# Splits of block sums one product sooner, seven-product pairs from pair 5 on, activation sums spread over pairs 2 to 4

## Chip, cores and metric

The kernel runs on one core of one Trainium2 chip. The metric is the device time of one execution in microseconds (us), as the median of several runs; lower is better.

## What is computed

A trunk of two layers on 512 tokens of width 1024. Each layer is a mixer sub-layer (four token mixers, gates, an output projection) followed by a gated feed-forward network. Only the second part is touched here:

```python
hf = rms_norm(x, norm_ffn_pre[l])
u = causal_depthwise_conv(hf @ ffn_w_up[l], ffn_conv_w[l], ffn_conv_b[l])   # width 3
gate, val = jnp.split(u, 2, axis=-1)
f = (jax.nn.gelu(gate, approximate=True) * val) @ ffn_w_down[l]
x = x + rms_norm(f, norm_ffn_post[l])
```

`ffn_w_up` is 1024 x 5632: 22 blocks of 128 gate columns and 22 of value columns.

## The kernel before

Every matrix product is made of three matmuls in a reduced float format: weight and activation are each split into a high and a low part (`whi`/`wlo`, `hT_hi`/`hT_lo`), and high x high, high x low and low x high are added up in PSUM. Splitting a weight tile of 128 x 1024 takes two instructions: a copy on ScalarE (ACT) that rounds to the high part, and a subtraction on VectorE (DVE) that leaves the low part. SyncE (SP) loads weights in the order of their use into three buffers `raw`; the split parts go to four buffers each.

The gate-and-value projection of a layer goes by **pairs**: pair i is gate block i and value block i. Pairs 0 and 1 come from `head`. A **whole pair** is two chains of 24 matmuls of 512 columns (tile `ps`). The pairs of the set `SEVEN` use a scheme of block sums instead, which needs seven products of quarter size where eight would be made (`seven`, L1401): each `product` is 12 matmuls of 256 columns into one of the banks `sa`, `sb`, `se`. It needs

- sums of the weights, made on GpSimd (POOL) in `w_seven` (four instructions per pair, L193 to L196) and then split by `halves` (L179 on ACT, L180 on DVE);
- sums of the activation, made once per layer by `forms`, for either half h of the contraction: `ta`, `tb`, `tc`, `td` on DVE (L1360), `te` on POOL (L1371 to L1373), and their splits `t1h`/`t1l` to `t4h`/`t4l` (L324 on ACT, L325 on DVE);
- copies of intermediate sums from a bank to SBUF on ACT (`ca` L1409 and L1416, `cb` L1422), since the next product adds on top of them in the same bank, and three additions on DVE (L1413, L1427, L1432).

Of a seven-product pair five products run in a row; the last two (`four`, `three`) are put off and run between the first products of the next pair (`more`). After each pair `ffn_pair` does the width-3 convolution: two ACT instructions (L1319), four DVE instructions (L1323), a GELU on ACT (L1327) and a product on DVE (L1331). From pair 4 on, each whole pair also splits some finished activations for the next stage (`split_act`, tiles `fh`, `fl`).

In this stage TensorE, ACT and DVE run in the order in which the program writes them, and POOL and SP in theirs; an instruction that waits holds up all behind it on its engine. `w_ahead(n)` writes the splits of the next n weights at that point. The instructions of `forms` are not written at once but queued in `bg`; `pump`, which is called after each product, writes some of them as long as DVE is reckoned to be less than a slack (0.9) behind TensorE. Before the first seven-product pair whatever is left in `bg` is written in one go:

```python
                if i in SEVEN:
                    while bg:
                        bg.popleft()()
                    seven(i)
                    continue
```

Of the kernel before, what the change touches and what calls it, by code (L numbers as in the profile page):

```python
# [21 lines left out]
NP_ = DFF // 128  # L22
# [58 lines left out]
T_G = 4.2  # L81
T_M = 5.7

SEVEN = {i for i in range(4, NP_ - 1) if i % 3}

H_2 = 1.0
H_T = 3.0
# [21 lines left out]
def build(tc, x, wts, prm, gains, cst, out, order=None):  # L109
# [4 lines left out]
    V, A, G, T, SP = nc.vector, nc.scalar, nc.gpsimd, nc.tensor, nc.sync  # L114
    with ExitStack() as ctx:
# [10 lines left out]
        def nm(s):  # L126
            uid[0] += 1
            return f"{s}{uid[0]}"

        def slot(w=512, dt=F32, name="g"):  # L130
            return pg.tile([128, w], dt, tag="g", bufs=NG, name=nm(name))
# [7 lines left out]
        def f(t):  # L139
            return t.bitcast(F32)  # L140
# [64 lines left out]
        def w_split(q, roomy=False):  # L205

            if recording:
                return
            while pos["spl"] <= min(q, len(order) - 1):
                i = pos["spl"]  # L210
                w_dma()
                w = unit_width(order[i][1])
                if order[i][1][0] == "fs":
                    w_seven(i)
                    pos["spl"] += 1
                    w_dma()
                    continue
                r = raw.pop(i)
                if roomy:
                    hs, ls = [], []  # L220
                    for c in range(0, w, 512):
                        n = min(512, w - c)
                        hi, lo = slot(dt=F32R, name="bh"), slot(dt=F32R, name="bl")
                        src = r[c // 512] if isinstance(r, list) else r[:, c:c + n]
                        A.activation(hi[:, :n], src, AF.Copy)
                        V.tensor_tensor(lo[:, :n], src, f(hi[:, :n]), op=ALU.subtract)
                        hs.append(hi)
                        ls.append(lo)
                    parts[i] = (hs, ls)
                else:  # L230
                    hi = pw.tile([128, WMAX], F32R, tag="whi", bufs=NSPL, name=nm("whi"))
                    lo = pw.tile([128, WMAX], F32R, tag="wlo", bufs=NSPL, name=nm("wlo"))
                    for c, s in ((0, r[0]), (512, r[1])) if isinstance(r, list) else ((0, r[:, :w]),):
                        n = 512 if isinstance(r, list) else w
                        A.activation(hi[:, c:c + n], s, AF.Copy)  # L235
                        V.tensor_tensor(lo[:, c:c + n], s, f(hi[:, c:c + n]), op=ALU.subtract)  # L236
                    parts[i] = (hi, lo)
                pos["spl"] += 1
                w_dma()

        def w_ahead(n=NSPL - 1):
            w_split(pos["use"] - 1 + n)

        def w_get(l, key):
            if recording:
                order.append((l, key))
                return nc, nc
            assert order[pos["use"]] == (l, key), (order[pos["use"]], key)
            w_split(pos["use"])
            p = parts.pop(pos["use"])  # L250
            pos["use"] += 1
            return p
# [7 lines left out]
        bg = deque()  # L260

        clk = {"pe": 0.0, "dve": 0.0, "slack": SLACK}
# [4 lines left out]
        def dve(us):  # L267
            clk["dve"] = max(clk["dve"], clk["pe"]) + us
# [50 lines left out]
        def hilo(src, scale=1.0, name="hl"):  # L319
            dve(0.62)  # L320
            hi = slot(dt=F32R, name=name + "h")
            lo = slot(dt=F32R, name=name + "l")
            if scale == 1.0:
                A.activation(hi, src, AF.Copy)  # L324
                V.tensor_tensor(lo, src, f(hi), op=ALU.subtract)  # L325
            else:
                A.activation(hi, src, AF.Copy, scale=scale)
                V.scalar_tensor_tensor(lo, src, scale, f(hi), op0=ALU.mult, op1=ALU.subtract)
            return hi, lo
# [269 lines left out]
        for l in range(L):  # L599
# [58 lines left out]
            for kv, b in enumerate((kcb, vcb)):  # L658
                for g in range(2):
                    t = slot(name="F")  # L660
# [674 lines left out]

            hb = head(l, [("fu", 0), ("fu", NP_), ("fu", 1), ("fu", NP_ + 1)], hooks)
            ffn_order.enter_context(tc.manual_schedule(engines={E_T, E_A, E_V}))
            clk["dve"] = clk["pe"]
            ffn_pair(0, hb[0:2])
            ffn_pair(1, hb[2:4])  # L1340
            hb = None
# [3 lines left out]
            def v2(t):  # L1345
                return t.rearrange("p (k t) -> p k t", k=2)
# [3 lines left out]
            def forms(h):  # L1350
                def block(t, k, q):
                    return f(t[:, k * 4 + h * 2:k * 4 + h * 2 + 2, q * 256:q * 256 + 256])
                hi, lo = (lambda k, q: block(hT_hi, k, q)), (lambda k, q: block(hT_lo, k, q))
                a, b, c, d, e, g = (slot(name="t" + n) for n in "abcdef")
                sub, add = ALU.subtract, ALU.add

                def op(o, x, y, how):
                    def go():
                        dve(0.62)
                        V.tensor_tensor(o, x, y, op=how)  # L1360
                    bg.append(go)
                op(v2(a), hi(0, 1), hi(0, 0), sub)
                op(v2(b), lo(0, 1), lo(0, 0), sub)
                op(a, a, b, add)
                op(v2(c), hi(1, 1), v2(a), sub)
                op(v2(c), v2(c), lo(1, 1), add)
                bg.append(lambda: form["d1"].append(hilo(a, name="t1")))
                op(v2(d), hi(1, 0), v2(c), sub)
                op(v2(d), v2(d), lo(1, 0), add)
                bg.append(lambda: form["d2"].append(hilo(c, name="t2")))  # L1370
                G.tensor_tensor(v2(e), hi(1, 1), hi(0, 1), op=sub)  # L1371
                G.tensor_tensor(v2(g), lo(1, 1), lo(0, 1), op=sub)
                G.tensor_tensor(e, e, g, op=add)  # L1373
                bg.append(lambda: form["d4"].append(hilo(d, name="t4")))
                bg.append(lambda: form["d3"].append(hilo(e, name="t3")))

# [6 lines left out]
            def product(b, w, c, n, first):  # L1383

                o = b[:, 0:256]
                kw = {} if first else {"skip_group_check": True}
                for kt in range(4):
                    hi, lo = side(n, kt)
                    k = c + kt * 128
                    mm(o, wc(w[0], k), hi, first and kt == 0, False, **kw)  # L1390
                    mm(o, wc(w[0], k), lo, False, False, **kw)
                    mm(o, wc(w[1], k), hi, False, kt == 3, **kw)
                pump(1.42)
# [3 lines left out]
            def more():  # L1397
                if rest:
                    rest.pop(0)()

            def seven(i):  # L1401


                ba, bb, be = bank("sa"), bank("sb"), bank("se")
                sa, sb = slot(name="ca"), slot(name="cb")
                L_, R_ = slice(0, 256), slice(256, 512)
                w0 = w_get(l, ("fs", i, 0))
                product(ba, w0, 0, (0, 0), True)
                A.activation(sa[:, L_], ba[:, L_], AF.Copy)  # L1409
                more()  # L1410
                w_ahead(2)
                product(bb, w0, 512, (1, 0), True)
                V.tensor_tensor(bb[:, L_], bb[:, L_], sa[:, L_], op=ALU.add)  # L1413
                w1 = w_get(l, ("fs", i, 1))
                product(ba, w1, 0, "d2", False)
                A.activation(sa[:, R_], ba[:, L_], AF.Copy)  # L1416
                w_ahead(2)
                more()
                product(be, w1, 512, "d1", True)
                w2 = w_get(l, ("fs", i, 2))  # L1420
                product(ba, w2, 0, "d3", False)
                A.activation(sb[:, L_], ba[:, L_], AF.Copy)  # L1422
                w_ahead()

                def four():
                    product(ba, w2, 512, "d4", False)
                    V.tensor_tensor(ba[:, R_], be[:, L_], sb[:, L_], op=ALU.add)  # L1427

                def three():
                    w3 = w_get(l, ("fs", i, 3))  # L1430
                    product(be, w3, 0, (1, 1), False)
                    V.tensor_tensor(bb[:, R_], be[:, L_], sa[:, R_], op=ALU.add)  # L1432
                    w_ahead(2)
                    ffn_pair(i, [bb, ba])
                rest.extend((four, three))

            forms(0)
            forms(1)
            for i in range(2, NP_):
                if i in SEVEN:  # L1440
                    while bg:
# [4 lines left out]
                for s in range(2):  # L1446
                    b = bank()
# [143 lines left out]
```

## Time and profile before

| | |
|---|---|
| median of 3 runs | 1943.7 us (1942.81 to 1944.19) |
| profiled execution, device time | 1941.42 us |
| its span | 1939.6 us |
| TensorE busy (matmul) | 1880.2 us, 97% of the span |
| VectorE busy | 1437.0 us, 74% |
| ScalarE busy | 955.6 us, 49% |
| GpSimd busy | 313.6 us, 16% |
| share of TensorE in the chain that ended last | 86% |
| up projection of layer 0 / layer 1 after `head` | 621 to 850 us / 1578 to 1808 us |

How to read it: times are from the start of the span. PE is TensorE, DVE VectorE, ACT ScalarE, POOL GpSimd, SP SyncE. A row of instructions gives line, engine, operation, "out<-in" by the program's names, sizes and the number of instructions merged; what stands in brackets at its end is the time that the engine stood idle before it and what ended that wait. The chain of waits follows the work that ended last back to its start. The granted clock is the share of full speed that TensorE ran at.

### The profile page before, as it was taken

The numbers are of one execution on the slowest core, as the hardware profiler recorded it, in microseconds if no ns is written. First come the engines' busy times: TensorE is split into PE (matmuls) and PEld (weight loads), VectorE is DVE, ScalarE is ACT, GpSimd is POOL, SyncE is SP. The second block draws the span as 40 slices with busy tenths as digits, with TensorE's granted clock in tenths as the row PEclk, the third lists the DMA queues.
The fourth block names the chain that finished last, engine by engine and source line by source line (L and its number), as shares of the span: only waits on it lengthen the run. The fifth ranks groups of instructions, "written<-read, shape, count | busy, mean of one in ns | idle before, by whom it ended". The sixth has DMA issues, their size and how long they took to land.

```text
span 1939.6 us, 27581 instructions
## 1 busy us (share of the span) xinstructions
PE 1880.2 (97%) x10236; PEld 1622.7 (84%) x10236; DVE 1437.0 (74%) x2546; ACT 955.6 (49%) x1840; POOL 313.6 (16%) x377
## 2 busy tenths in 40 slices
PE   8999999999999799999999999999999997999997
PEld 7988888888888789988898888888888897899886
DVE  6898779797557887873468987897975587787622
ACT  5557577623344455553345666775233444555521
POOL 1403300000004143400023033000000052243000
PEclk9999999999999899999999999999999998999999
DMA  8523311222353123344454233122323521232432
GB/s 291 157 77 98 109 50 55 77 94 86 103 162 133 56 87 106 101 134 130 150 189 148 66 104 109 50 62 71 97 81 113 206 79 60 88 109 89 140 119 77
DMA packets 74696, 209.10 MB, mean 108 GB/s; under 512 B 11073, under 2 KB 11457, under 8 KB 74561
## 3 DMA queue, kind: packets, MB, share of 16 engines
q1 hardware_dynamic: 67392, 192.65, 30.7%
q0 software_dynamic: 7168, 14.69, 3.0%
q8 instruction: 80, 1.31, 0.3%
q14 instruction: 56, 0.45, 0.1%
HBM read 184.23 MB, written 8.39 MB: 99 GB/s over the span
## 4 chain that ended last, share of the span: by engine, by line
PE 86%; DVE 9%; issue 2%; ACT 1%; DMA 1%; POOL 0%; SPq 0%; DVEq 0%; POOLq 0%; ACTq 0%
PE ps L296 45%; PE tk L296 16%; PE sa L296 5%; PE hd L296 5%; PE o L296 3%; PE se L296 3%; DVE wlo L180 3%; DVE fu L1323 2%; PE vt L296 2%; PE sB L296 1%; PE sA L296 1%; PE sb L296 1%; PE tr L385 1%; DVE fu L1331 1%; PE tB L1076 1%
## 5 line engine op out<-in xcount | busy, mean ns | idle before, releaser
L235 ACT ACTIVATE whi<-raw 128x1024 fp32r<-128x1024 f32 (+2 forms) x270 | 254.3, 947 | 461.0 <-PE ps L296 258.5
L236 DVE TENSOR_TENSOR wlo<-raw,whi 128x1024 fp32r<-128x1024 f32 (+2 forms) x270 | 297.3, 1105 | 229.3 <-ACT whi L235 227.5
L296 PE MATMUL ps<-hT_hi,whi 128*128 128x512 f32 x1104 | 437.5, 396 | 0.8 <-DVE ob L1095 0.8
L296 PE MATMUL ps<-hT_hi,wlo 128*128 128x512 f32 x1104 | 435.0, 394 | 0.0
L296 PE MATMUL ps<-hT_lo,whi 128*128 128x512 f32 x1104 | 433.3, 393 | 0.0
L296 PEld LDWEIGHTS ps<-hT_hi,wlo 128*128 128x128 f32 x1104 | 207.6, 188 | 46.5
L296 PEld LDWEIGHTS ps<-hT_hi,whi 128*128 128x128 f32 x1104 | 207.8, 188 | 43.3 <-DVE ob L1095 1.7
L296 PEld LDWEIGHTS ps<-hT_lo,whi 128*128 128x128 f32 x1104 | 207.8, 188 | 42.5
L898 DVE SCALAR_TENSOR_TENSOR acc<-ct,prm,acc 128x511 f32<-128x511 f32 (+14 forms) x240 | 175.5, 731 | 3.4
L296 PE MATMUL tk<-whi,fh 128*128 128x512 f32 x336 | 130.9, 390 | 0.0
L296 PE MATMUL tk<-whi,fl 128*128 128x512 f32 x336 | 130.7, 389 | 0.0
L296 PE MATMUL tk<-wlo,fh 128*128 128x512 f32 x336 | 130.7, 389 | 0.0
L351 POOL TENSOR_TENSOR sm<-sm,mhalf 128x1 f32<-128x1 f32 x32 | 22.2, 694 | 547.8 <-DVE sm L350 547.8
L180 DVE TENSOR_TENSOR wlo<-raw,whi 128x1024 fp32r<-128x1024 f32 x48 | 73.7, 1536 | 35.2 <-ACT whi L179 35.2
L1055 ACT ACTIVATE P<-P,sm 128x256 f32<-128x256 f32 (+3 forms) x128 | 70.6, 554 | 29.7 <-DVE sm L1053 28.0
L932 POOL TENSOR_TENSOR sm<-sm,mhalf 128x1 f32<-128x1 f32 x8 | 6.1, 762 | 479.6 <-DVE sm L930 472.5
L193 POOL TENSOR_TENSOR s<-raw 128x512 f32<-128x512 f32 x24 | 39.3, 1637 | 260.1 <-DMA raw<-wts 254.2
L296 PEld LDWEIGHTS tk<-wlo,fh 128*128 128x128 f32 x336 | 63.1, 188 | 13.1
L296 PEld LDWEIGHTS tk<-whi,fl 128*128 128x128 f32 x336 | 63.1, 188 | 13.1
L296 PEld LDWEIGHTS tk<-whi,fh 128*128 128x128 f32 x336 | 63.1, 188 | 13.0
L580 POOL DMA_DIRECT2D Q<-hlh x64 | 31.6, 497 | 198.9 <-ACT hlh L324 189.8
L296 PE MATMUL hd<-hT_hi,bh 128*128 128x256 f32 x256 | 63.4, 285 | 0.0
(352 smaller groups left out, 4591.5 us busy)
## 6 DMA issues: line engine op xcount, KB each, us to landing
raw<-wts SPq DMA_DIRECT2D x260, 512.0 KB, 3.5
raw<-wts SPq DMA_DIRECT2D x66, 256.0 KB, 2.6
br<-wts SPq DMA_DIRECT2D x40, 256.0 KB, 6.2
xr<-x SPq DMA_DIRECT2D x16, 256.0 KB, 5.0
gain<-gains SPq DMA_DIRECT2D x16, 256.0 KB, 6.2
Q<-hlh POOLq DMA_DIRECT2D x64, 64.0 KB, 2.4
Q<-hll POOLq DMA_DIRECT2D x64, 64.0 KB, 3.1
raw<-wts SPq DMA_DIRECT2D x8, 408.0 KB, 5.1
```

The source lines that it names most:

```text
L180: V.tensor_tensor(lo[:, c:c + n], s, f(hi[:, c:c + n]), op=ALU.subtract)
L193: G.tensor_tensor(s1, r2[:, 0:512], r2[:, 512:1024], op=ALU.add)
L235: A.activation(hi[:, c:c + n], s, AF.Copy)
L236: V.tensor_tensor(lo[:, c:c + n], s, f(hi[:, c:c + n]), op=ALU.subtract)
L296: T.matmul(o, lhsT=lhsT, rhs=rhs, start=start, stop=stop, **kw)
L351: G.tensor_tensor(v[:, 1:2], v[:, 0:1], mhalf[:, 0:1], op=ALU.pow)
L385: T.transpose(bs[t, h][:, k * 128:k * 128 + 128], y[h][:, k * 128:k * 128 + 128], ident)
L580: G.dma_start(f(dst[row:row + 32, :]), f(src[srow:srow + 32, :]))
L898: V.scalar_tensor_tensor(acc[i][:, k:], ct[i][:, :512 - k], w[:, 30 - k:31 - k], acc[i][:, k:], op0=ALU.mult, op1=ALU.add)
L1055: A.activation(P[i], P[i], AF.Exp, bias=mn[:, i:i + 1], scale=-1.0, accum_out=sm[:, i:i + 1])
L1076: T.transpose(B[j][:, (i - j) * 128:(i - j) * 128 + 128], P[i][:, j * 128:j * 128 + 128], ident)
L1323: V.scalar_tensor_tensor(us[s][:, d:], bs[s][:, :512 - d], w(2 - d, s), us[s][:, d:], op0=ALU.mult, op1=ALU.add)
```

## The change

- `SEVEN` was pairs 4, 5, 7, 8, 10, 11, 13, 14, 16, 17, 19, 20 (12 pairs); it is now 5, 6, 8, 9, 11, 12, 14, 15, 17, 18, 20 (11 pairs). Whole pairs are 2, 3, 4, 7, 10, 13, 16, 19, 21 instead of 2, 3, 6, 9, 12, 15, 18, 21. Since `split_act` is called in whole pairs with a growing target, two activations are split in each of pairs 4, 7 and 10, where it was four in pair 6 and two in pair 9.
- The reckoning of DVE's lag is set to zero after the convolutions of pairs 0 and 1, not before them, so `pump` begins earlier to write the activation sums.
- `te` is made from `tc` with two POOL instructions instead of three from the inputs, and is queued like the others.
- In `seven`, splits are written one product sooner, and the last `w_ahead` of `three` is left out.

```diff
-SEVEN = {i for i in range(4, NP_ - 1) if i % 3}
+SEVEN = {i for i in range(5, NP_ - 1) if i % 3 != 1}
...
             hb = head(l, [("fu", 0), ("fu", NP_), ("fu", 1), ("fu", NP_ + 1)], hooks)
             ffn_order.enter_context(tc.manual_schedule(engines={E_T, E_A, E_V}))
-            clk["dve"] = clk["pe"]
             ffn_pair(0, hb[0:2])
             ffn_pair(1, hb[2:4])
...
+                bg.append(lambda: (G.tensor_tensor(v2(e), v2(c), hi(0, 0), op=sub),
+                                   G.tensor_tensor(v2(e), v2(e), lo(0, 0), op=sub)))
                 op(v2(d), hi(1, 0), v2(c), sub)
                 op(v2(d), v2(d), lo(1, 0), add)
                 bg.append(lambda: form["d2"].append(hilo(c, name="t2")))
-                G.tensor_tensor(v2(e), hi(1, 1), hi(0, 1), op=sub)
-                G.tensor_tensor(v2(g), lo(1, 1), lo(0, 1), op=sub)
-                G.tensor_tensor(e, e, g, op=add)
...
                 w0 = w_get(l, ("fs", i, 0))
+                w_ahead(1)
                 product(ba, w0, 0, (0, 0), True)
                 A.activation(sa[:, L_], ba[:, L_], AF.Copy)
+                w_ahead(2)
                 more()
-                w_ahead(2)
                 product(bb, w0, 512, (1, 0), True)
                 V.tensor_tensor(bb[:, L_], bb[:, L_], sa[:, L_], op=ALU.add)
                 w1 = w_get(l, ("fs", i, 1))
+                w_ahead(2)
                 product(ba, w1, 0, "d2", False)
                 A.activation(sa[:, R_], ba[:, L_], AF.Copy)
-                w_ahead(2)
+                w_ahead()
                 more()
...
                     V.tensor_tensor(bb[:, R_], be[:, L_], sa[:, R_], op=ALU.add)
-                    w_ahead(2)
                     ffn_pair(i, [bb, ba])
                 rest.extend((four, three))
 
+            clk["dve"] = clk["pe"]
             forms(0)
             forms(1)
```

Three places show what this does to the order. The first is DVE just after the convolution of pair 1 (`fu<-hd`), layer 0. Before:

```order
L1323 SCALAR_TENSOR_TENSOR fu_6350<-hd_6099,prm_119,fu_6350 128x510
L236 TENSOR_TENSOR wlo_6392<-raw_6204,whi_6391 128x1024
L1331 TENSOR_TENSOR fu_6342<-fu_6341,fu_6342 128x512
L1331 TENSOR_TENSOR fu_6350<-fu_6349,fu_6350 128x512
L180 TENSOR_TENSOR wlo_6427<-raw_6210,whi_6426 128x1024
L1360 TENSOR_TENSOR ta_6357<-hT_hi 128x512
L1360 TENSOR_TENSOR tb_6358<-hT_lo 128x512
L1323 SCALAR_TENSOR_TENSOR fu_6450<-ps_6375,prm_119,fu_6450 128x511
```

Now:

```order
L1323 SCALAR_TENSOR_TENSOR fu_6350<-hd_6099,prm_119,fu_6350 128x510
L1359 TENSOR_TENSOR ta_6357<-hT_hi 128x512
L1359 TENSOR_TENSOR tb_6358<-hT_lo 128x512
L236 TENSOR_TENSOR wlo_6386<-raw_6204,whi_6385 128x1024
L1359 TENSOR_TENSOR ta_6357<-ta_6357,tb_6358 128x512
L1359 TENSOR_TENSOR tc_6359<-hT_hi,ta_6357 128x512
L1331 TENSOR_TENSOR fu_6342<-fu_6341,fu_6342 128x512
L1331 TENSOR_TENSOR fu_6350<-fu_6349,fu_6350 128x512
L1359 TENSOR_TENSOR tc_6359<-tc_6359,hT_lo 128x512
L236 TENSOR_TENSOR wlo_6424<-raw_6210,whi_6423 128x1024
L325 TENSOR_TENSOR t1l_6433<-ta_6357,t1h_6432 128x512
L1359 TENSOR_TENSOR td_6360<-hT_hi,tc_6359 128x512
```

Seven instructions of the sums stand there before pair 2's own convolution, where it was two.

The second place is DVE ahead of the first addition of the first seven-product pair (`sb<-sb,ca`). Before, fifteen instructions of the sums stand between pair 3's convolution and that addition, four for the first half and eleven for the second; the last ten of them:

```order
L1360 TENSOR_TENSOR tb_6367<-hT_lo 128x512
L1360 TENSOR_TENSOR ta_6366<-ta_6366,tb_6367 128x512
L1360 TENSOR_TENSOR tc_6368<-hT_hi,ta_6366 128x512
L1360 TENSOR_TENSOR tc_6368<-tc_6368,hT_lo 128x512
L325 TENSOR_TENSOR t1l_6557<-ta_6366,t1h_6556 128x512
L1360 TENSOR_TENSOR td_6369<-hT_hi,tc_6368 128x512
L1360 TENSOR_TENSOR td_6369<-td_6369,hT_lo 128x512
L325 TENSOR_TENSOR t2l_6563<-tc_6368,t2h_6562 128x512
L325 TENSOR_TENSOR t4l_6567<-td_6369,t4h_6566 128x512
L325 TENSOR_TENSOR t3l_6571<-te_6370,t3h_6570 128x512
L1413 TENSOR_TENSOR sb_6575<-sb_6575,ca_6577 128x256
```

Now, after the last convolution of pair 4:

```order
L1323 SCALAR_TENSOR_TENSOR fu_6623<-ps_6587,prm_119,fu_6623 128x510
L325 TENSOR_TENSOR t1l_6631<-ta_6362,t1h_6630 128x512
L1359 TENSOR_TENSOR td_6365<-hT_hi,tc_6364 128x512
L1359 TENSOR_TENSOR td_6365<-td_6365,hT_lo 128x512
L325 TENSOR_TENSOR t2l_6639<-tc_6364,t2h_6638 128x512
L325 TENSOR_TENSOR t4l_6643<-td_6365,t4h_6642 128x512
L325 TENSOR_TENSOR t3l_6647<-te_6366,t3h_6646 128x512
L1412 TENSOR_TENSOR sb_6651<-sb_6651,ca_6653 128x256
```

Six of them are left at that place.

The third place is ACT from the first copy of a seven-product pair that follows a whole pair (pair 7 before, pair 8 now). Before:

```order
L1409 ACTIVATE ca_6932<-sa_6929 128x256
L1327 ACTIVATE fu_6921<-fu_6921 128x512
L1416 ACTIVATE ca_6932<-sa_6929 128x256
L179 ACTIVATE whi_6975<-raw_6791 128x1024
L1422 ACTIVATE cb_6933<-sa_6929 128x256
```

Now:

```order
L1408 ACTIVATE ca_7000<-sa_6997 128x256
L179 ACTIVATE whi_7029<-raw_6867 128x1024
L1327 ACTIVATE fu_6989<-fu_6989 128x512
L1416 ACTIVATE ca_7000<-sa_6997 128x256
L179 ACTIVATE whi_7056<-s_7034 128x512
L179 ACTIVATE whi_7056<-s_7033 128x512
L1422 ACTIVATE cb_7001<-sa_6997 128x256
```

The split of the next pair's first weight now stands ahead of the GELU and of the second copy, and the split of its sums ahead of the third.

## Rows read from the trace of the kernel before

**Rows 1.** First part of the page: TensorE's busy time and share

```profile
PE 1880.2 (97%) x10236; PEld 1622.7 (84%) x10236; DVE 1437.0 (74%) x2546; ACT 955.6 (49%) x1840; POOL 313.6 (16%) x377
```

**Rows 2.** Timeline of TensorE: matmuls that began after a wait, both layers

```profile
656.83 0.58 PE L296 MATMUL sa<-t2h,whi 128*128 128x256 f32 x1 [11.04 <-ACT ca L1409]
...
696.30 0.39 PE L296 MATMUL sa<-t3h,whi 128*128 128x256 f32 x1 [3.22 <-ACT ca L1416]
...
698.81 0.38 PE L296 MATMUL sa<-hT_hi,wlo 128*128 128x256 f32 x1 [0.57 <-DVE wlo L180]
...
728.73 0.39 PE L296 MATMUL sa<-t3h,whi 128*128 128x256 f32 x1 [0.32 <-ACT ca L1416]
...
731.96 0.39 PE L296 MATMUL sa<-hT_hi,wlo 128*128 128x256 f32 x1 [1.30 <-DVE wlo L180]
...
794.74 0.39 PE L296 MATMUL sa<-hT_hi,wlo 128*128 128x256 f32 x1 [0.48 <-DVE wlo L180]
...
1611.82 0.58 PE L296 MATMUL sa<-t2h,whi 128*128 128x256 f32 x1 [9.47 <-ACT ca L1409]
...
1646.35 0.38 PE L296 MATMUL sa<-t2h,wlo 128*128 128x256 f32 x1 [0.84 <-DVE wlo L180]
...
1652.71 0.39 PE L296 MATMUL sa<-t3h,whi 128*128 128x256 f32 x1 [3.20 <-ACT ca L1416]
```

**Rows 3.** Chain of waits: start, us, what; up projection of both layers

```profile
620.98 11.01 PE ps L296 x48
...
656.83 2.93 PE sa L296 x12
659.76 1.81 PE se L296 x12
...
668.73 2.86 PE se L296 x24
...
698.81 2.88 PE sa L296 x22
...
1611.82 2.93 PE sa L296 x12
1614.76 2.15 PE se L296 x12
...
1655.23 3.74 PE sa L296 x22
```

**Rows 4.** Stages: us, busy time of each engine, granted clock, DMA

```profile
643.00:657.00 14.00, 2.96 (x25) 2.75 (x24) 13.60 (x22) 5.35 (x10) 0.00 (x0) 0.76 0.13 38
1644.00:1680.00 36.00, 31.93 (x203) 28.80 (x202) 30.09 (x37) 17.09 (x30) 11.55 (x8) 0.95 0.27 88
```

**Rows 5.** Timeline of DVE, pairs 2 to 4 of layer 0

```profile
628.56 1.21 DVE L180 TENSOR_TENSOR wlo<-raw,whi 128x1024 fp32r<-128x1024 f32 x1
...
632.83 1.53 DVE L1323 SCALAR_TENSOR_TENSOR fu<-ps,prm,fu 128x511 f32<-128x511 f32 x2 [0.41 <-ACT fu L1319]
634.28 3.18 DVE L180 TENSOR_TENSOR wlo<-s,whi 128x512 fp32r<-128x512 f32 x2
...
653.32 0.68 DVE L325 TENSOR_TENSOR t1l<-ta,t1h 128x512 fp32r<-128x512 f32 x1
...
654.63 0.69 DVE L1360 TENSOR_TENSOR td<-td,hT_lo 128x512 f32<-128x512 f32 x1
```

**Rows 6.** Timeline of POOL, first and last of four sums for pair 5

```profile
633.92 1.30 POOL L193 TENSOR_TENSOR s<-raw 128x512 f32<-128x512 f32 x1 [5.83 <-issue]
...
638.58 1.75 POOL L195 TENSOR_TENSOR s<-raw,s 128x512 f32<-128x512 f32 x1
```

**Rows 7.** Timeline of ACT after whole pair 15

```profile
789.64 0.63 ACT L1327 ACTIVATE fu<-fu 128x512 f32<-128x512 f32 x1 [0.88 <-DVE fu L1323]
791.18 0.38 ACT L1416 ACTIVATE ca<-sa 128x256 f32<-128x256 f32 x1 [0.91 <-PE sa L296]
791.46 1.05 ACT L179 ACTIVATE whi<-raw 128x1024 fp32r<-128x1024 f32 x1
```

More of the change, by code (lines that the diff above doesn't have):

```diff
@@ L1353, in forms @@
                 hi, lo = (lambda k, q: block(hT_hi, k, q)), (lambda k, q: block(hT_lo, k, q))
-                a, b, c, d, e, g = (slot(name="t" + n) for n in "abcdef")
+                a, b, c, d, e = (slot(name="t" + n) for n in "abcde")
                 sub, add = ALU.subtract, ALU.add
```

## Prediction

> **What bounds the kernel now.** I read the page first: TensorE is busy 97% of the span [rows 1], so a gain can only be time in which TensorE waits, runs slowly, or does work that falls away. Then TensorE's timeline over the two up projections, which gives each wait above 0.1 us [rows 2]; where a wait recurs, one row stands there and the count here. In layer 0 the first seven-product pair (4) waits 11.04 us in front of its third product, for the copy `ca` that stands behind the activation sums on ACT. Pair 7, the first after a whole pair with four activation splits, waits 3.22 and 0.57. Pair 10, the first after a whole pair with two such splits, waits 0.32 and 1.30. Of the three later triplets (one whole pair, two seven-product pairs) two wait 0.48 each. Sum: 17.4 us. Layer 1 has 9.47, then 0.84 and 3.20, then the rows of pair 10 again (within 0.01), then 0.48 three times: 16.6 us.
>
> The chain of waits shows what such a wait costs besides. A product takes 1.43 us at full speed (two in 2.86), but the first product after the 11.04 us took 2.93 and the next 1.81; in layer 1, 2.93 and 2.15; and after 0.84 and 3.20, 22 matmuls took 3.74 where 22 took 2.88 after 3.22 and 0.57 in layer 0 [rows 3]. A mean granted clock of 0.76 in the stage with the wait, 0.95 in that of pair 7 in layer 1 [rows 4] says why: part of it ran at 1.2 instead of 2.4 GHz. Cost: (2.93 + 1.81 - 2.86) = 1.9, (2.93 + 2.15 - 2.86) = 2.2, and 0.9.
>
> **a. One seven-product pair becomes a whole pair.** A whole pair takes 11.01 us, seven products 7 x 1.43 = 10.0 [rows 3]. +1.0 per layer, **+2.0**.
>
> **b. The activation sums.** They now run in the gaps of pairs 2 to 4. Does DVE finish in time? By the clock of layer 0, pair 2 begins at 620.98 and three whole pairs end at 654.0; two products later, at 656.85, pair 5's third product is due and needs the copy. By the new order six instructions of the sums are still left behind pair 4's convolution, of which `t1l`, `td`, `td` stand ahead of the ACT chain `t4h`, `t3h`, `ca`. Pair 2's chain ended at 631.99, its last convolution began at 632.83 and the next instruction at 634.28 [rows 3, 5]: 0.84 and 1.45 us. `t1l` to the end of the second `td` takes 2.00 (653.32 to 655.32), and from there TensorE resumed after 1.51 (656.83) [rows 2, 5]. So at best 654.0 + 0.84 + 1.45 + 2.00 + 1.51 = 659.8: a wait of **2.95**, not nothing.
>
> Two things add to it. The first is POOL. Its four sums for pair 5 took from 633.92 to 640.33 [rows 6], 6.4 us where four times the undisturbed 1.30 is 5.2, and beside them two DVE subtractions of 512 took 3.18 where two take about 1.3 [rows 5]. That is about 0.95 us of DVE for each POOL instruction beside it. `te` now waits for `tc`, so it and then pair 6's four sums fall just behind `tc` of the second half: beside pair 4's convolution and this chain. Three contended instructions: +2.85.
>
> The second is what DVE carries in. A weight's subtraction takes 1.14 start to start (1.21 less the overlap of rows), a 512-wide one 0.60 to 0.71, I take 0.64. From the end of one whole pair's last convolution to the start of the next one's there are 11.01 - 1.45 = 9.55 us. Pair 2's gap gets nine of 512, two of 1024 and one convolution of 1.45: 9.5, so it is full. Pair 3's gets six, two and one, 7.6 (2.0 free); pair 4's nine, one and one, 8.35 (1.2 free). POOL adds two `te` in pair 2 and some 2.5 of pair 5's sums in pair 3, 4.5 x 0.95 = 4.3. Carried: 4.3 - 3.2 = 1.1.
>
> I take 2.95 + 2.85 + 1.1 = **6.9 us** in either layer. Ends: 2.95 if POOL is never in the way; the present 9.47 to 11.04 if all of it is. The clock's drop stays (1.9 and 2.2), since 9.47 brought it and in layer 1 even 0.84 and 3.20 did; the single 3.22 in layer 0 did not. So b is 2 x 6.9 - (11.04 + 9.47) = **-6.7**.
>
> On this point the Trainium skill has a rule (SBUF — State Buffer, "Who interferes with whom"): DVE instructions with two inputs in SBUF and GpSimd instructions that read SBUF share an exclusive port, and the one that comes second waits for the whole of the other. The rows show 0.95 per POOL instruction, not its full 1.30. By the rule the wait would be about 9.4 in place of 6.9; that is a rival below.
>
> **c. Four activation splits become two, and two are moved into pair 4.** The two in pair 4 are counted above. Pair 7 now has two, as pair 9 had, so pair 8 should wait as pair 10 did: 0.32 + 1.30 = 1.62 per layer instead of 3.79 and 4.04, and without the clock's 0.9. Pair 10 also has two, so pair 11 takes over the old 1.62. c: 2 x 1.62 - 3.79 - 4.04 - 0.9 = **-5.5**.
>
> **d. Splits one product sooner.** On ACT the first seven-product pair of a triplet now has a weight copy of 1.05 ahead of the GELU and the copy `ca`. ACT stands idle 0.88 in front of that GELU and 0.91 in front of `ca` [rows 7], 1.8 together, which hide it. On the other side nothing TensorE waits for comes sooner: the waits of 1.30 and 0.48 are for a subtraction on DVE, whose order there is the same as before. If DVE were relieved, at most those go: 2 x 2 x 1.62 + 5 x 0.48 = 8.9. I take **0**, nearer to ACT's idle rows. SP's weight loads keep their order and follow the buffers; they can only start sooner. The two POOL instructions fewer were run beside `head`, where TensorE had no wait: 0. The last `w_ahead` of `three` is covered by the one in front of it: 0.
>
> **Sum.** 2.0 - 6.7 - 5.5 + 0 = -10.2. The profiled execution took 1941.42 us (span 1939.6), 2.3 under the median of the runs. 1941.4 - 10.2 = 1931.2 there, and **1933.5** against the median of 1943.7. A measurement of this kernel can tell 0.2% from no change, about 4 us: below 1939.8 is faster, above 1947.6 slower.
>
> **Rivals.**
> 1. POOL is not in the way (its instructions fall beside convolutions, which read PSUM). Pair 5 waits 2.95, the clock stays up as after 3.22: 2 x (2.95 - 6.9) - 4.1 = -12.0 more, 1921.5. For it: DVE has 3 us free in pairs 3 and 4. Against: `te` and pair 6's sums are queued just where the last chain runs.
> 2. POOL holds DVE up for its whole instruction, as in the rule named above. The chain costs 3 x 1.3 = 3.9, the carry 4.5 x 1.3 - 3.2 = 2.6, the wait 9.45: 2 x 2.55 = +5.1, 1938.6.
> 3. The change doesn't do what it says: the work only moves one pair on, and pair 5 waits as long as pair 4 did. The 6.7 of b are lost: 1940.2, within 0.2%. For it: pair 2's gap is full, and pair 4 gets two splits more.
> 4. Slower: the split's copy on ACT stands in front of `ca`, on which TensorE's next product in that bank depends, in all 22 seven-product pairs. If the copy starts so late (raw weight or buffer not yet free) that more than the 1.8 us idle is used up, each pair is held by up to that copy: 22 x 1.05 = +23, 1956.6. Against: the idle time just read, and weights that POOL has already read by then.
>
> **How the numbers follow.** Forecast 0.45 (1933.5), rival 1 0.28, rival 2 0.12, rival 3 0.08, rival 4 0.07. The forecast, rivals 1 and 2 are faster; with a little taken off for rival 2, which lies at the border: faster 0.83, same 0.10, slower 0.07. The range goes from a little under rival 1 (1920) to just over rival 3 (1941) and leaves out rival 4 and the tails.
>
> **What would show it.** a: 11 pairs with `se` per layer. b: a wait for `ca` in pair 5 of 6 to 8 us with a slow product after it; POOL's sums beside `t1l` and `td`, and these at 1.6 us each instead of 0.65. c: pair 8 waits some 1.6 us. d: no wait of TensorE for `ca` L1416 behind a weight copy. It is wrong if pair 5 waits under 4 or over 10 us, or if new waits of about 1 us recur in each triplet.

## The result, and the profile after

The changed kernel took **1957.13 us** (1956.72 to 1957.89, four runs) where the kernel before, run on the same chip, took 1943.26 (1942.15 to 1944.19, four runs). The ratio is 1.0072 with a 95% interval of 1.0055 to 1.009: 13.9 us slower, where 10.2 faster was forecast. The profiled execution took 1957.09 us (span 1955.2).

From the first and fourth part of the page (busy time by engine; shares of the chain that ended last):

```profile
PE 1889.5 (97%) x10164; PEld 1624.2 (83%) x10164; DVE 1460.4 (75%) x2534; ACT 951.4 (49%) x1828; POOL 297.9 (15%) x365
PE 79%; DVE 13%; issue 4%; ACT 4%; DMA 0%; POOL 0%; SPq 0%; DVEq 0%; POOLq 0%; ACTq 0%
```

Set it beside [rows 1]. DVE has 12 instructions fewer and is busy 23.4 us longer; POOL has 12 fewer too and is busy 15.7 less. TensorE's share of the chain fell from 86 to 79%, DVE's rose from 9 to 13%. So DVE's instructions got longer, and TensorE waits for them.

TensorE's waits, grouped by what ended them, over the up projection of layer 0 (total, times, longest):

```profile
PE se L296 <- DVE sa L1427: 6.7, 5, 1.6
PE sa L296 <- ACT ca L1408: 6.6, 1, 6.6
PE sa L296 <- ACT ca L1416: 6.0, 4, 2.1
PE sa L296 <- DVE wlo L180: 2.2, 4, 0.6
```

The wait of the first seven-product pair fell from 11.04 and 9.47 [rows 2] to 6.6 in both layers, near the 6.9 that was forecast. The group that ends with the addition L1427 did not exist before: 6.7 us here and 4.9 in layer 1, 11.6 in all. The waits add up to 21.5 and 19.0 us, where they were 17.4 and 16.6: **+6.5**.

The timeline of TensorE answers to [rows 2]; the first row is pair 5, the next the whole pair 7, the last pair 8:

```profile
662.19 0.58 PE L296 MATMUL sa<-t2h,whi 128*128 128x256 f32 x1 [6.63 <-ACT ca L1408]
...
686.77 0.36 PE L296 MATMUL se<-hT_hi,whi 128*128 128x256 f32 x1 [1.18 <-DVE sa L1427]
...
702.71 0.39 PE L296 MATMUL sa<-t3h,whi 128*128 128x256 f32 x1 [2.12 <-ACT ca L1416]
```

The second and third row come back, with other lengths, in the five triplets of a layer: a wait for L1427 when the put-off product `three` wants to add to the bank `se` that this addition still reads (0.8 to 1.6 us), and then, in all but the last triplet, two or three in the next pair. The chain of waits of layer 0 shows how the second comes about, and what it does to TensorE:

```profile
662.19 2.93 PE sa L296 x12
665.12 1.97 PE se L296 x12
667.10 4.29 PE sa L296 x36
...
695.69 4.53 DVE wlo L180 x3
700.22 0.67 DVE fu L1323
...
701.76 0.63 ACT fu L1327
702.71 6.28 PE sa L296 x36
...
740.43 6.20 PE sa L296 x36
```

Three subtractions of splits on DVE (two of 512, one of 1024) take 4.53, the convolution and the GELU behind them come late, and `ca` L1416 stands behind the GELU on ACT. After the waits of 2.1 us 36 matmuls took 6.28 and 6.20 instead of 4.29; a like row in layer 1 took 6.05. That is 2.0 + 1.9 + 1.8 of reduced clock. The kernel before had one such place, pair 7 of layer 1. Its 22 matmuls in 3.74 [rows 3] are not all of it: 14 others of the same 36 stand ahead of them in the chain.

```profile
1652.71 2.50 PE sa L296 x14
```

So the 36 took 6.24 there, which is 2.0 above 4.29, and not the 0.9 that the prediction took from the 22 alone. With pair 5 (2.93 + 1.97 here, and 2.93 + 2.56 in layer 1) the clock now cost about 10.3 us, where it was 1.9 + 2.2 + 2.0 = 6.1: **+4.2**. Together with the part that a whole pair more costs, 2.0 + 6.5 + 4.2 = 12.7, against 15.7 between the two profiled executions; 3.0 us are not located.

Where do DVE's long instructions come from? DVE at whole pair 16, from the convolution of pair 14, which is put off that far, to the addition L1427 of pair 15; the first row is the subtraction just before it:

```profile
785.83 1.23 DVE L236 TENSOR_TENSOR wlo<-raw,whi 128x1024 fp32r<-128x1024 f32 x1 [1.18 <-ACT whi L235]
...
788.24 1.54 DVE L1323 SCALAR_TENSOR_TENSOR fu<-sb,prm,fu 128x511 f32<-128x511 f32 x2 [0.85 <-ACT fu L1319]
789.69 1.53 DVE L1323 SCALAR_TENSOR_TENSOR fu<-sa,prm,fu 128x511 f32<-128x511 f32 x2
791.14 1.48 DVE L180 TENSOR_TENSOR wlo<-s,whi 128x512 fp32r<-128x512 f32 x1
792.54 2.31 DVE L236 TENSOR_TENSOR wlo<-raw,whi 128x1024 fp32r<-128x1024 f32 x1
794.78 1.77 DVE L1331 TENSOR_TENSOR fu<-fu,fu 128x512 f32<-128x512 f32 x1
796.47 0.42 DVE L1427 TENSOR_TENSOR sa<-se,cb 128x256 f32<-128x256 f32 x1
```

and POOL in the same stretch, first and last of its four sums:

```profile
790.77 1.30 POOL L193 TENSOR_TENSOR s<-raw 128x512 f32<-128x512 f32 x1 [15.95 <-DMA raw<-wts]
...
795.96 1.72 POOL L195 TENSOR_TENSOR s<-raw,s 128x512 f32<-128x512 f32 x1
```

The two convolution rows, which read PSUM, have their usual length. The three instructions behind them have both inputs in SBUF and run beside POOL's sums: 1.48, 2.31 and 1.77 instead of 0.68, 1.22 and 0.69. Together that is 3.0 us more, and L1427 comes late by it. Of the 66 subtractions `wlo<-s` of the two layers, which take 0.68 when nothing is in their way, 26 took over 0.8 us; in the kernel before it was 8 of 72. In [rows 5] and [rows 6] the same thing happened at another place, and cost TensorE nothing there.

### The profile page after: what moved, and what is told of

Read it like the earlier page. It is cut to its first block, busy times and chain, and to the rows that moved or that the text cites. A ratio compares the mean times of both kernels' runs of the same rounds, so it can differ in the third digit from the quotient of the medians.

```text
span 1955.2 us, 27377 instructions
## 1 busy us (share of the span) xinstructions
PE 1889.5 (97%) x10164; PEld 1624.2 (83%) x10164; DVE 1460.4 (75%) x2534; ACT 951.4 (49%) x1828; POOL 297.9 (15%) x365
## 3 DMA queue, kind: packets, MB, share of 16 engines
q8 instruction: 80, 1.31, 0.3%
## 4 chain that ended last, share of the span: by engine, by line
PE 79%; DVE 13%; issue 4%; ACT 4%; DMA 0%; POOL 0%; SPq 0%; DVEq 0%; POOLq 0%; ACTq 0%
PE ps L296 41%; PE tk L296 16%; PE hd L296 5%; PE sa L296 4%; DVE wlo L180 3%; PE o L296 3%; DVE fu L1323 3%; PE vt L296 2%; DVE wlo L236 1%; DVE fu L1331 1%; PE sB L296 1%; ACT fu L1319 1%; PE sA L296 1%; PE sb L296 1%; PE tr L385 1%
## 5 line engine op out<-in xcount | busy, mean ns | idle before, releaser
L236 DVE TENSOR_TENSOR wlo<-raw,whi 128x1024 fp32r<-128x1024 f32 (+2 forms) x274 | 306.8, 1124 | 245.0 <-ACT whi L235 243.4
L296 PE MATMUL ps<-hT_hi,whi 128*128 128x512 f32 x1136 | 450.0, 396 | 0.8 <-DVE ob L1095 0.8
L296 PE MATMUL ps<-hT_hi,wlo 128*128 128x512 f32 x1136 | 447.4, 394 | 0.0
L296 PE MATMUL ps<-hT_lo,whi 128*128 128x512 f32 x1136 | 446.2, 393 | 0.0
L296 PEld LDWEIGHTS ps<-hT_hi,wlo 128*128 128x128 f32 x1136 | 213.6, 188 | 47.8
L296 PEld LDWEIGHTS ps<-hT_hi,whi 128*128 128x128 f32 x1136 | 213.9, 188 | 45.0 <-DVE ob L1095 1.7
L296 PEld LDWEIGHTS ps<-hT_lo,whi 128*128 128x128 f32 x1136 | 213.9, 188 | 43.7
L180 DVE TENSOR_TENSOR wlo<-s,whi 128x512 fp32r<-128x512 f32 x66 | 65.5, 1019 | 6.0 <-ACT whi L179 6.0
L180 DVE TENSOR_TENSOR wlo<-raw,whi 128x1024 fp32r<-128x1024 f32 x44 | 65.3, 1484 | 0.0
L296 PE MATMUL hd<-hT_hi,bl 128*128 128x256 f32 x256 | 62.0, 280 | 0.0
```

The costliest lines, as they stand in the source:

```text
L296: T.matmul(o, lhsT=lhsT, rhs=rhs, start=start, stop=stop, **kw)
```

## The experiments

Two theories stood at the start. **P**: the sooner splits make POOL's weight sums run beside DVE's subtractions, and those hold TensorE up. **O**: the new order on ACT and DVE holds it up by itself, whatever POOL does (this is the fourth rival's thought).

**1. The old places of the splits in the changed kernel.** In `seven`, all else as changed (a `-` is the changed kernel):

```diff
                 w0 = w_get(l, ("fs", i, 0))
-                w_ahead(1)
...
-                w_ahead(2)
                 more()
+                w_ahead(2)
...
                 w1 = w_get(l, ("fs", i, 1))
-                w_ahead(2)
...
-                w_ahead()
+                w_ahead(2)
...
                     V.tensor_tensor(bb[:, R_], be[:, L_], sa[:, R_], op=ALU.add)
+                    w_ahead(2)
```

> The changed kernel with the splits in a seven-product pair written where they were before; 11 such pairs and the activation sums in the gaps stay. Theory P (sooner splits free the weight buffers sooner, so POOL's sums start some 2 us sooner and fall beside DVE subtractions instead of beside convolutions): the waits of `se` for the addition L1427 (11.6 us over both layers) and the larger waits in pairs 8 and 11 go; about 1933 us, as the prediction had it without the splits. Rival O (the order itself: on DVE the next weight's subtraction stands ahead of the addition L1432): about 1933 too. Rival S (the other set of pairs, or two activation splits in each of three pairs): stays near 1957.

Measured: 1929.88 us (1929.24 to 1931.24), ratio to before 0.9933 (0.9918 to 0.9948). So all that is not the place of the splits made the kernel 13.3 us faster, and the place of the splits cost 1957.1 - 1929.9 = **27.2 us**. S falls; P and O had both expected about 1933. TensorE's waits in layer 0 (lines are two or so lower than in the changed kernel):

```profile
PE sa L296 <- ACT ca L1407: 6.6, 1, 6.6
PE sa L296 <- DVE wlo L180: 3.6, 4, 1.3
PE sa L296 <- ACT ca L1414: 0.6, 2, 0.3
```

No wait for the addition (L1425 here) is left, and one of the 66 subtractions `wlo<-s` took over 0.8 us, where it was 26. Over both layers the waits add up to 22.3 us instead of 40.6. DVE and POOL at the same place of the program as above, whole pair 16:

```profile
777.36 1.21 DVE L236 TENSOR_TENSOR wlo<-raw,whi 128x1024 fp32r<-128x1024 f32 x1
778.50 1.53 DVE L1323 SCALAR_TENSOR_TENSOR fu<-sb,prm,fu 128x511 f32<-128x511 f32 x2
...
781.38 0.68 DVE L180 TENSOR_TENSOR wlo<-s,whi 128x512 fp32r<-128x512 f32 x1
781.98 1.22 DVE L236 TENSOR_TENSOR wlo<-raw,whi 128x1024 fp32r<-128x1024 f32 x1
783.11 0.69 DVE L1331 TENSOR_TENSOR fu<-fu,fu 128x512 f32<-128x512 f32 x1
783.72 0.43 DVE L1425 TENSOR_TENSOR sa<-se,cb 128x256 f32<-128x256 f32 x1
```

```profile
783.13 1.82 POOL L193 TENSOR_TENSOR s<-raw 128x512 f32<-128x512 f32 x1 [15.53 <-DMA raw<-wts]
```

From the convolution to the addition the DVE instructions and their order are the same. POOL begins 4.6 us after the convolution here and 2.5 after it in the changed kernel, and that is enough: addition 5.2 us after the convolution's start, not 8.2. POOL starts when the second of two raw weight transfers has landed, and SP issues these when raw buffers come free, here when DVE's subtraction of an earlier weight has ended. SP's two issues in the changed kernel:

```profile
784.67 0.33 SPq L168 DMA_DIRECT2D raw<-wts  x1
...
787.08 0.33 SPq L168 DMA_DIRECT2D raw<-wts  x1
```

and with the old places of the splits:

```profile
777.14 0.33 SPq L168 DMA_DIRECT2D raw<-wts  x1
...
778.60 0.33 SPq L168 DMA_DIRECT2D raw<-wts  x1
```

The second issue stands just behind the end of the subtraction L236 in both kernels (787.06 and 778.57). Here DVE's order did change: the sooner split puts this subtraction, of the next whole pair's weight, ahead of the addition L1432 of the pair before, and it was behind it. Measured from the copy L1416 of pair 15 (784.46 and 774.52), the second issue stands at 2.6 instead of 4.1 us, and its transfer took less time: POOL began 3.7 us after it instead of 4.5. Why it landed faster was not tested; the two issues stand 2.4 us apart there, and 1.5 here. POOL's start moved from 8.6 to 6.3. The swap held nothing up by itself: the addition L1432 (L1430 here) starts 2.5 us behind the copy in both, and the convolution no later.

**2. The new places of the splits in the kernel before**, the same edit the other way round and nothing else of the change.

> The kernel before with only the splits written one product sooner; 12 seven-product pairs, sums as before. P and O: slower than before by 15 to 30 us (waits for L1427 in each whole pair, 6 per layer at about 1.2, and larger waits behind the copy L1416). S: within 4 us of before.

Measured: 1966.91 us (1965.53 to 1967.83), ratio 1.0124 (1.0107 to 1.0141): +23.7 by themselves, with the same signature in layer 0 (five waits for the addition, where the expectation had six):

```profile
PE se L296 <- DVE sa L1429: 6.5, 5, 1.4
...
PE sa L296 <- ACT ca L1418: 5.5, 4, 2.1
```

**3 to 5. POOL without its reads.** The four sums of `w_seven` are left out; three fills, which write a tile and read none, stand in their place, so that the block sums of the weights are not computed. Edited so: the changed kernel (3), the kernel before (4), and the kernel of experiment 1 (5).

```diff
-                G.tensor_tensor(s1, r2[:, 0:512], r2[:, 512:1024], op=ALU.add)
-                G.tensor_tensor(s2, s1, r1[:, 0:512], op=ALU.subtract)
-                G.tensor_tensor(s4, r1[:, 512:1024], s2, op=ALU.subtract)
-                G.tensor_tensor(r2[:, 0:512], r1[:, 0:512], r2[:, 0:512], op=ALU.subtract)
+                for s in (s1, s2, s4):
+                    G.memset(s, 0.0)
```

> The changed kernel with POOL's four sums per seven-product pair left out and three constant fills in their place, so that POOL reads nothing there (the sums of weights are therefore not computed). P: the waits for L1427 vanish, pair 8 and 11 wait under 0.5, about 1925 us. O and S: the waits for L1427 stay at about 1 us in each triplet, above 1948.

> The same left out in the kernel before (sums of weights not computed): what POOL's reads cost there. P: the waits of 1.62 and 0.48 go and pair 4's wait shrinks by 2 to 4 us in either layer, 1925 to 1933 us. O and S: within 3 us of before.

> The splits where they were before (as in the first experiment) and POOL's four sums left out for three fills (sums of weights not computed). With the changed kernel and the same left out at 1909.5 us, this closes the table of two by two. P (sooner splits cost only by way of POOL's reads): 1909 within 4 us. O (the order on DVE and ACT itself costs): below 1900, since the 27 us that the splits cost beside POOL should show here too in part.

Measured, one run each: 1909.46, 1924.31 and 1908.24 us. POOL's sums cost the kernel before 19 us, that of experiment 1 21.6, and the changed kernel 47.7. With them gone the place of the splits makes 1909.46 - 1908.24 = 1.2 us, of the 27.2 with them: O falls. Two expectations were missed. Experiment 3 came out 16 us under its 1925: pair 5's wait shrank too, and those of the later pairs went altogether. In experiment 4, which ends 0.7 under its range, pair 4's wait shrank by 2.1 us in layer 0 but only by 0.5 in layer 1. Leaving the sums out also makes their results ready at once; but in the changed kernel no wait of TensorE, ACT, DVE or SP in the two up projections ended with a POOL instruction, and POOL's share of the chain is 0%, so it was not late sums that cost the time. In 3 and 5 the only wait above 0.1 us left in either up projection is that of pair 5, at the same length in both; its row in experiment 3:

```profile
659.01 0.58 PE L294 MATMUL sa<-t2h,whi 128*128 128x256 f32 x1 [2.99 <-ACT ca L1406]
```

**6. The changed kernel with POOL a little later.** Nothing of the order on ACT and DVE is touched; ahead of the sums of one pair of each triplet POOL does a sum of one column, which waits for the weight, and four fills (0.53 us each):

```diff
                 s1, s2, s4 = slot(name="s1"), slot(name="s2"), slot(name="s4")
+                if p % 3 == 2:
+                    G.tensor_tensor(s1[:, 0:1], r2[:, 0:1], r2[:, 512:513], op=ALU.add)
+                    for _ in range(4):
+                        G.memset(s1, 0.0)
```

> The changed kernel, splits sooner as in it, with one tiny sum that waits for the weight and four constant fills of 0.53 us ahead of POOL's first sum in the first seven-product pair after a whole pair, so that these sums start some 2.5 us later, where they started before (8.6 us behind the second pair's copy L1416 instead of 6.3); the fills read nothing. P: the waits of `se` for the addition L1427 go, 1930 to 1938 us. O: no change, 1957, or slower.

Measured: 1933.54 us (1933.28 to 1935.65), ratio 0.995 (0.9933 to 0.9966). Waits of layer 0:

```profile
PE sa L300 <- ACT ca L1412: 8.8, 1, 8.8
PE sa L300 <- ACT ca L1420: 2.9, 2, 1.4
PE sa L300 <- DVE wlo L180: 2.1, 4, 0.6
```

DVE's first convolution row and its addition, and POOL's first sum, in whole pair 13 (in whole pair 16 both distances are 5.2 us):

```profile
748.48 1.53 DVE L1327 SCALAR_TENSOR_TENSOR fu<-sb,prm,fu 128x511 f32<-128x511 f32 x2 [0.85 <-ACT fu L1323]
...
753.71 0.42 DVE L1431 TENSOR_TENSOR sa<-se,cb 128x256 f32<-128x256 f32 x1
```

```profile
753.86 1.30 POOL L197 TENSOR_TENSOR s<-raw 128x512 f32<-128x512 f32 x1
```

Work added to POOL took 23.6 us off the kernel. POOL now begins 5.4 us after the convolution, the addition comes 5.2 after it, and the waits for it are gone. What is lost against experiment 1 is mostly pair 5, whose sums were held back as well: it waits 8.77 and 8.69 instead of 6.59 and 6.83, 4.0 in all, and 1933.5 - 4.0 = 1929.5 is close to experiment 1's 1929.9. (Pairs 8 and 11 wait about 1.1 us more in all than there, which this sum leaves out.)

**7. One split of the four put back.** The split behind the second copy takes two weights again, and `three` has its `w_ahead(2)`; the earlier ones stay as changed.

```diff
                 A.activation(sa[:, R_], ba[:, L_], AF.Copy)
-                w_ahead()
+                w_ahead(2)
...
                     V.tensor_tensor(bb[:, R_], be[:, L_], sa[:, R_], op=ALU.add)
+                    w_ahead(2)
```

> The changed kernel with two of its five moves undone: the split of the next whole pair's first weight stands again behind the addition L1432 (in `three`), the other splits sooner. P: that weight's buffer carries the second raw weight of the next pair; its transfer starts at the old time, POOL's sums some 1 to 1.5 us later than in the changed kernel, and the waits for L1427 shrink to under 0.4: 1932 to 1942 us. O: the subtraction no longer stands ahead of the addition: about 1930.

Measured: 1942.48 us in one run, 0.5 above the range of P and 12 above what O expected. Half of the loss is back: no wait for L1427 is left, POOL begins 4.0 us after the convolution (whole pair 13). But the other waits of pairs 8 and 11 stayed: 2.53 each in layer 0, and 3.50 and 3.21 in layer 1. Pair 8 in layer 0:

```profile
701.79 0.58 PE L296 MATMUL sa<-t3h,whi 128*128 128x256 f32 x1 [2.53 <-ACT ca L1416]
```

The second sums of a triplet still fall beside subtractions of splits. DVE and then POOL, at pair 14:

```profile
765.42 2.33 DVE L180 TENSOR_TENSOR wlo<-raw,whi 128x1024 fp32r<-128x1024 f32 x1
767.68 2.96 DVE L1323 SCALAR_TENSOR_TENSOR fu<-ps,prm,fu 128x511 f32<-128x511 f32 x4
```

```profile
764.86 1.81 POOL L193 TENSOR_TENSOR s<-raw 128x512 f32<-128x512 f32 x1 [3.62 <-DMA raw<-wts]
766.75 2.16 POOL L194 TENSOR_TENSOR s<-s,raw 128x512 f32<-128x512 f32 x1
768.87 1.30 POOL L196 TENSOR_TENSOR raw<-raw,raw 128x512 f32<-128x512 f32 x1
```

**8. Experiment 1 with pair 6's sums held back.** In pair 5 three instructions of the last activation chain ran beside POOL's sums for pair 6. These now wait for `te` (`held[0]`, set where `forms` makes it) and for ten fills; the diff is against experiment 1:

```diff
+                if p == 6:
+                    te = held[0]
+                    G.tensor_tensor(s1[:, 0:1], te[:, 0:1], te[:, 1:2], op=ALU.add)
+                    for _ in range(10):
+                        G.memset(s1, 0.0)
```

> The kernel of the first experiment (old places of the splits), with ten fills of 0.53 us on POOL behind `te` and ahead of pair 6's sums, so that nothing reads on POOL beside `t1l`, `td`, `td`. By the prediction's terms pair 5's wait falls by 2.85 to about 3.7 us in either layer and the clock may stay up: 1929.9 - 5.7 (- 4) = 1920 to 1925 us. If the wait is DVE's own backlog: stays at 6.6, 1930 us.

Measured: 1923.61 us (1922.54 to 1924.31), ratio 0.9898 (0.9884 to 0.9913). Pair 5 waits 3.83 and 4.28:

```profile
659.04 0.58 PE L302 MATMUL sa<-t2h,whi 128*128 128x256 f32 x1 [3.83 <-ACT ca L1414]
```

This version computes everything and is faster than both kernels, by 1% and 1.7%. Moving the second sums of each triplet was not tried.

## Why the prediction was wrong, point by point

**a and b, right.** Pair 5 waited 6.63 and 6.56 where 6.9 was forecast (6.59 and 6.83 in experiment 1), and its three parts can be told apart. Without POOL's reads the wait was 2.99 (2.95 forecast as the part that no contention makes). The three instructions beside POOL, in the changed kernel's timeline of DVE:

```profile
655.61 1.74 DVE L325 TENSOR_TENSOR t1l<-ta,t1h 128x512 fp32r<-128x512 f32 x1
657.27 1.75 DVE L1359 TENSOR_TENSOR td<-hT_hi,tc 128x512 f32<-128x512 f32 x1
659.05 1.63 DVE L1359 TENSOR_TENSOR td<-td,hT_lo 128x512 f32<-128x512 f32 x1
```

are as long as [rows 5] led to expect, and holding POOL back took 2.8 off the wait in layer 0 and 2.6 in layer 1 (2.85 forecast). What is then left above 2.99 is 0.84 and 1.29 (1.1 forecast).

**c, right without d, but for its clock.** In experiment 1 pair 8 waited 0.33 + 1.31 = 1.64 in layer 0 and 1.67 in layer 1; 1.62 was forecast. Pair 8 ran at full speed behind these waits (in layer 1 22 matmuls in 2.89), so what the clock gave back is the whole 2.0 of pair 7 in the kernel before, and not 0.9. a to c together were forecast at -10.2 and measured at -13.3; 1.1 of the 3 us between them is this term, and the other 2 were not traced to a place.

**d is the step that failed.** The prediction set it at 0, with two reasons: "a subtraction on DVE, whose order there is the same as before", and "SP's weight loads keep their order and follow the buffers; they can only start sooner". The second is true, and led on from there the wrong way: "sooner" was taken for harmless. A sooner split frees a raw buffer sooner, the transfer into it is issued sooner, and POOL's sums, which are released by that transfer, move 2.3 us towards DVE's subtractions. The first is true from the convolution on; before it the subtraction L236 moved ahead of the addition L1432, and that is what freed the second buffer sooner. Where DVE's order stayed, its durations did not. The prediction had the price of this meeting, 0.95 us per POOL instruction, and used it for pair 5; it did not use it for the later pairs, whose POOL sums the splits move. The late additions and convolutions became waits, and TensorE's clock was lower behind several of them, 27.2 us in all. Of the 27.9 us between the profiled executions of the changed kernel and of experiment 1, 18.3 are waits (40.6 against 22.3) and about 6 are the clock (10.3 against 4.3, all of it in pair 5); the rest is not located. The prediction named its own sign of error, new waits of about 1 us in each triplet, and they came.

**The rivals.** Rival 4 gave 1956.6, within 1 us of the result, by a mechanism that did not act: experiment 6 leaves ACT's copies where they are and runs in 1933.5. Its agreement with the result is chance. Rival 3 fell, since pair 5 did not wait as pair 4 had. Rival 1 would have needed POOL out of the way: pair 5 waited 2.99 only without POOL's sums. Rival 2 fell by its size: it had pair 5 wait 9.45. On its rule: the Trainium skill (SBUF — State Buffer, "Who interferes with whom") says that only instructions which use the port pair shared by DVE and GpSimd get in each other's way, and that the pair is held as a lock. The trace agrees on who is hit: the convolutions, which read PSUM, took 2.96 us for four beside POOL (experiment 7), as they did with POOL idle (2.97 at 644.46 in the kernel before), and instructions with two inputs in SBUF grew. They grew by 0.8 to 1.1 us each (1.48 for 0.68, 2.31 for 1.22, 1.77 for 0.69), less than the 1.30 of an undisturbed POOL instruction that rival 2 took.

## What to carry to other kernels

When an edit lets something happen sooner, follow the buffer that it frees: which transfer starts on it, which engine that transfer releases, and beside what that engine's work then falls. An instruction order that stays the same says nothing of its durations when a second engine can get in its way. And a helper engine that is 15% busy may still set the time: here it paid to hold it back with fills, and to let its work fall where the other helper reads PSUM or stands idle.

## What was not expected

- POOL's four sums per pair cost 19 us in the kernel before and 47.7 in the changed one, though the one makes them for 24 pairs and the other for 22: where they fall, not how many they are, makes the difference.
- POOL's fills do not slow DVE: in experiment 8, the second `td` and the three subtractions `t2l`, `t4l` and `t3l` behind it took 0.68 to 0.69 us each while ten fills ran from 656.32 to 662.09.
- TensorE's clock fell behind some short waits and not behind others. After the 2.12 us in front of pair 8, 36 matmuls took 6.28 where 4.29 is full speed; the granted clock of that stretch was 0.73, so part of it ran at 1.2 GHz. In the kernel before, the 3.22 us in layer 0 were followed by full speed [rows 3], and the 3.20 us in layer 1, which came after a wait of 0.84 [rows 2], by 36 matmuls in 6.24. In the changed kernel smaller waits (1.18 and 0.56) came shortly before pair 8's; but in layer 1 the same 2.11 in pair 8, after 0.86 and 0.24, left the granted clock at 1.00. What decides stays open.
